# Layer A's dilated keys and group 0's values through DRAM, with GpSimd issuing the moves

## The chip, the cores and the metric

One core of a Trainium2 chip runs the kernel. Its engines are TensorE (PE: matmuls, and transposes as matmuls against an identity), VectorE (DVE), ScalarE (ACT), GpSimd (POOL) and SyncE (SP, which here only issues DMA transfers). Each works through its own instructions in order and waits on semaphores for the others. The metric is the time of one execution on the device in microseconds.

## The reference

Two encoder layers on x (512 tokens, 1024 channels, 16 heads of 64). Each layer is

```
hn = rms_norm(x, norm_gain[i]);  x = x + mixer(hn)
```

Layer A is dilated sliding-window attention: `hn @ w_in` gives, for each of three groups g with dilation 1, 4 and 16, queries, keys and values for all heads, and a gate besides.

```
for g in 0, 1, 2:
    q = rms_norm(qkv[g, 0], q_gain[g]);  k = rms_norm(qkv[g, 1], k_gain[g]);  v = qkv[g, 2]
    # keys at offsets 0, +-d, .., +-reach*d;  reach*d = 64, 256, 1024
    logits = q k^T / 8 + t5_bias;   o_g = softmax(logits) v;   lse_g = log of its denominator
y = sum_g softmax_g(lse_g) * o_g
return (y * silu(gate)) @ w_out
```

Layer B is a two-dimensional neighbourhood attention on an 8 x 64 grid (window 8 x 16, one group) with the same frame. The change is in layer A alone.

## The kernel before

**Tiling.** Every product of a weight with activations is split in two fp32r parts (`wh`, `wl` for the weight, `hn_h`, `hn_l` for the activation) and made of three matmuls (`mm3`). Weights come from DRAM as tiles `wraw` of 1024 columns (three buffers). `split` (L128 to L134) casts each half of one to `wh` on ScalarE and subtracts to `wl` on GpSimd for two tiles in five and on VectorE for the rest; `wh` and `wl` have four buffers each.

**Order.** A layer is a loop over eight pairs of heads, `hc` 0 to 7. `main()` yields TensorE's projections for each pair: first keys and values of groups 1 and 2 (`rawk`, with the values in `v12`), then the three groups' queries and group 0's key (`rawq`), group 0's values (`v0_a`) and the gate (`gate_a`). `side()` holds the attention: `k_a`, `q_a`, `v_a`, `attn_a`. `run` interleaves the two by a clock that counts the nominal time of TensorE's matmuls (213 ns for 512 columns): a side step is taken when its due time, in those nanoseconds after a stamp, has come. `later_on(delay, job)` puts a job on the same clock. TensorE's order is exactly the order of this program (`manual_schedule`); what the other engines do is ordered by a scheduler, except for instructions that `keep_in_program_order` pins.

**Steps that the change touches.**
- `project_qk` copies each accumulator out of PSUM on ScalarE (L477), `squares` squares it on GpSimd (L282, L284) and sums it on VectorE, `head_norm` scales by the root on VectorE (L307), for `rawk` of pairs 1 to 6 by a job 9000 ns later.
- `k_a` transposes the keys of groups 1 and 2 on TensorE, four 128 x 128 transposes a group (L213), and VectorE scales the result into `k12` (L544). `v_a` does the same for group 0's values (`vt`), which ScalarE copies to `v0` (L632).
- For pairs 0 to 5 (`moved`) queries and group 0's key take another way (`turn_q`, `move_q`): VectorE transposes blocks of 32 x 32 in place, SyncE writes the tile to DRAM (`qd`, L595) and reads it back in four parts in which the blocks stand in their new places (`qt`, L601). `split_q` makes the two fp32r parts of query and key.
- In `attn_a` the scores of a pair come in two halves, u = 0 and 1, then the softmax: VectorE minima, ScalarE exponentials (L831) and scaling (L672). The probabilities go back transposed (P^T) in the manner of the queries: `turner.put` transposes blocks on VectorE (L744), `turner.send` writes them to DRAM (`td`, L753) and reads four parts (`pt`, L757), on SyncE. `weigh` multiplies P^T with the values one pair later.
- Pair 6 moves P^T but transposes its queries on TensorE; pair 7 transposes all on TensorE. Layer B uses `turner` too.

Of the kernel before, what the change touches and what calls it, by code (L numbers as in the profile page):

```python
# [42 lines left out]
def tile_hybrid_encoder(  # L43
# [234 lines left out]
    def squares(v, ss, i, ns):  # L278
        sq = wk.tile([P, 512], F32, tag="sq", name="sq")[:, : ns * 64]
        if len(v.shape) == 3:  # L280
            v = v.rearrange("p (a f) r -> p a f r", f=4)
            nc.gpsimd.tensor_mul(sq.rearrange("p (f a r) -> p a f r", f=4, a=4), v, v)  # L282
# [8 lines left out]
    def head_norm(raw, ss, ns, held, delay=0):  # L291


        rs = wk.tile([P, 32], F32, tag="rs", name="rs")
        rsqrt(nc.vector if ns == 8 else nc.gpsimd, rs[:, : 4 * ns], ss[:, : 4 * ns], 4 * ns, 1.0 / DH)

        def scale():
            for i in range(4):
                by = rs[:, i * ns : (i + 1) * ns].unsqueeze(2)
                if len(raw.shape) == 4:  # L300
                    v = raw[:, :, i, :].rearrange("p (h a f) r -> p f h a r", h=2, f=4)
                    by = rs[:, i * ns : (i + 1) * ns].rearrange("p (f h) -> p f h", h=2)
                    by = by.unsqueeze(3).unsqueeze(4).to_broadcast([P, 4, 2, 2, 32])
                else:
# [34 lines left out]
    rs_n = cp.tile([P, 4], F32, name="rs_n")  # L339
    rs_trj = cp.tile([P, S], F32, name="rs_trj")  # L340
    rs_half = cp.tile([P, S], F32, name="rs_half")
# [45 lines left out]
    def scales_a():  # L387
        pa = spread()
        nc.scalar.mul(tjr(rs_half), to_tjr(pa), 0.5)
        nc.scalar.copy(trj(rs_trj), to_trj(pa))  # L390

# [49 lines left out]

    def part(n):
        return rk[:, 1024 * n : 1024 * n + 1024].rearrange("p (i c) -> p i c", i=4)

    def project_qk(n, ns, key, hc, guard, first=False, **kw):
# [3 lines left out]
        def evac(i, acc):  # L449
            if not box:  # L450
# [7 lines left out]
                elif key == "rawk":  # L458
                    box.append(part(0))
                    st["v12", hc] = part(1 + hc % 3)  # L460
                else:
# [7 lines left out]
            elif key == "rawk":  # L469
                pieces = [(raw[:, i, :], acc[:, :256]), (st["v12", hc][:, i, :], acc[:, 256:])]  # L470
            else:
                pieces = [(raw[:, i, :], acc[:, :n])]
            for dst, src in pieces:
                if first:
                    nc.scalar.copy(dst, src)
                else:
                    nc.scalar.activation(dst, src, AF.Copy, scale=rs_n[:, i : i + 1])  # L477
            if not first:
                squares(raw[:, :, i, :] if key == "rawq" and moved(hc) else raw[:, i, : ns * 64], ss, i, ns)

# [8 lines left out]
    def normed(raw, ss, ns, key, hc):  # L489
        head_norm(raw, ss, ns, key == "raw", 9000 if key == "rawk" and 0 < hc < NHC - 1 else 0)  # L490
        if key == "rawq" and moved(hc):
            turn_q(raw)
        st[key, hc] = raw
        stamp[key, hc] = clock[0]

    def first_out():

        raw, ss = st.pop("first")
        for i in range(4):
            for t in (raw, st["v12", 0]):  # L500
                nc.scalar.activation(t[:, i, :], t[:, i, :], AF.Copy, scale=rs_n[:, i : i + 1])
            squares(raw[:, i, :], ss, i, 4)
        normed(raw, ss, 4, "rawk", 0)
# [12 lines left out]
    def v0_a(hc):  # L516
# [3 lines left out]
        vt = wk.tile([P, EXT], F32, tag="vt", name="vt", bufs=1)  # L520
        nc.vector.tensor_mul(trj(vt[:, 64:EXT]), to_trj(acc[0]), trj(rs_trj))
        nc.gpsimd.tensor_copy(vt[:, 0:64], vt[:, EXT - 64 : EXT])
        st["vt", hc] = vt
        stamp["vt", hc] = clock[0]
# [13 lines left out]
    def k_a(hc):  # L538
        yield "wait", ("rawk", hc), 12500 if hc == 0 else 22500 if hc < NHC - 1 else 10000
        k12 = wk.tile([P, 2, 512], F32, tag="k12", name="k12", bufs=1)  # L540
        raw = st.pop(("rawk", hc))
        for g in range(2):
            tp = transpose4(raw, g * P)
            nc.vector.tensor_scalar(k12[:, g, :], tp, gk[:, g + 1 : g + 2], None, op0=ALU.mult)  # L544
            yield
        st["k12", hc] = k12, st.pop(("v12", hc))
        stamp["k12", hc] = 0

    def turn_q(raw):
# [66 lines left out]

    def split_q(q0h, q0l, qt, k0h, k0l):
        src = qt[:, :, 3, :].rearrange("p t (j r) -> p t r j", j=4)
        trj4 = lambda t: t[:, 64:EXT].rearrange("p (t r j) -> p t r j", t=4, j=4)
        tc.keep_in_program_order(nc.scalar.copy(trj4(k0h), src))  # L620
        by_t = lambda t: t.rearrange("p (t x) -> p t x", t=4)
        put_k([(by_t(q0h), by_t(q0l), qt[:, :, 0, :])], 0, True)
        nc.vector.tensor_sub(trj4(k0l), src, trj4(k0h.bitcast(F32)))

    def v_a(hc):
# [4 lines left out]
        for i in range(4):  # L630
            transpose(tp[:, i * P : (i + 1) * P], vt[:, i * P : (i + 1) * P])
        nc.scalar.copy(v0[hc % 2], tp.rearrange("p (i c) -> p i c", i=4))  # L632
        stamp["v", hc] = 0
# [99 lines left out]
    class turner:  # L733
# [11 lines left out]

        def send(self, dst, wait, pace):

# [4 lines left out]
            src = self.t[:, : 4 * run].rearrange("p (b x) -> p b x", b=4)  # L752
            tc.keep_in_program_order(nc.sync.dma_start(d.rearrange("b p x -> p b x"), src))  # L753

            def read(b):
                src = d[b].rearrange("(a k) x -> k a x", a=4)
                tc.keep_in_program_order(nc.sync.dma_start(place[32 * b : 32 * b + 32], src))  # L757
                self.left -= 1
# [4 lines left out]
    def attn_a(hc):  # L763
# [7 lines left out]
        def scores(u):  # L771
# [381 lines left out]
    def side():  # L1153
# [23 lines left out]
        for hc in range(NHC):  # L1177
            if hc < NHC - 1:
                yield from k_a(hc)
                yield from chain(q_a(hc), v_a(hc))  # L1180
                if moved(hc):
                    yield from st.pop(("land", hc))
                yield from attn_a(hc)
                if hc == 1:
# [114 lines left out]
```

## Time and profile before

| | |
|---|---|
| time, median of 3 runs | 851.97 us (850.87 to 852.74) |
| the profiled execution | 852.44 us |
| its span, first to last instruction | 850.6 us |
| TensorE busy | 842.8 us (99%) |
| VectorE, ScalarE, GpSimd busy | 518.5, 431.5, 309.8 us |
| DMA | 141.23 MB, mean 166 GB/s |

The span of the profiled execution is 1.8 us shorter than its time. A matmul's busy time overlaps with the next one's, so a busy TensorE is not one at its peak; what a group of instructions costs is read from the starts of its neighbours. Issuing a DMA does not count as busy. Names such as `acc<-wh,hn_h` mean output and inputs; L209 is the line of the helper through which all matmuls go, L213 that of the transposes.

### The profile page before, as it was taken

What the parts mean: (1) busy time and instruction counts of PE and PEld (TensorE: products, weight loads), DVE (VectorE), ACT (ScalarE), POOL (GpSimd) and SP (SyncE); (2) the same over time, 40 slices, a digit from 0 to 9 for tenths busy, and PEclk for the clock granted to TensorE, in tenths of its full rate; (3) what the DMA queues carried; (4) which work ended last, traced back from release to release, by engine and by line L of the source; (5) the groups of instructions that cost most, each with busy time, mean ns of one, the idle gap of its engine ahead of it and who ended that gap; (6) DMA issues with size and microseconds to landing.
All of it is one profiled execution on the core that took longest, in us unless ns stands there. A gap on an engine that the chain in (4) does not pass through costs nothing.

```text
span 850.6 us, 15397 instructions
## 1 busy us (share of the span) xinstructions
PE 842.8 (99%) x5546; PEld 702.5 (83%) x5546; DVE 518.5 (61%) x1336; ACT 431.5 (51%) x923; POOL 309.8 (36%) x494
## 2 busy tenths in 40 slices
PE   9999999999999999999999999999999999999998
PEld 7788878788788788788788787789998898889786
DVE  7354684684674674674675745447567656766642
ACT  7433653653653653652653554355366655665531
POOL 2252441542541541542531341121354335542511
PEclk9999999999999999999999999999999999999999
DMA  7346377477478378378375562264245664555333
GB/s 250 110 126 216 97 228 227 137 226 241 128 227 248 102 228 243 102 230 246 99 236 159 147 191 79 60 241 146 82 143 138 174 175 148 168 163 158 99 97 127
DMA packets 65228, 141.23 MB, mean 166 GB/s; under 512 B 5760, under 2 KB 23104, under 8 KB 65152
## 3 DMA queue, kind: packets, MB, share of 16 engines
q1 hardware_dynamic: 65008, 139.99, 54.5%
q8 instruction: 44, 0.72, 0.3%
q10 hardware_dynamic: 144, 0.26, 0.1%
q14 instruction: 32, 0.26, 0.1%
HBM read 109.11 MB, written 31.12 MB: 165 GB/s over the span
## 4 chain that ended last, share of the span: by engine, by line
PE 94%; ACT 3%; DVE 1%; DMA 1%; issue 0%; DVEq 0%; ACTq 0%
PE acc L209 80%; PE log L209 5%; PE o L209 5%; PE tp L213 3%; ACT p L1084 1%; ACT p L672 1%; DMA x_all<-in_xt 0%; ACT p L831 0%; ACT wh L128 0%; DVE hn_l L397 0%; ACT rawk L477 0%; DMA eb<-lb_d 0%; PE pa L209 0%; PE pl L209 0%; DVE p L820 0%
## 5 line engine op out<-in xcount | busy, mean ns | idle before, releaser
L128 ACT CAST wh<-wraw 128x512 fp32r<-128x512 f32 (+1 forms) x275 | 161.4, 588 | 294.7 <-PE acc L209 258.0
L209 PE MATMUL acc<-wh,hn_h 128*128 128x512 f32 (+1 forms) x768 | 293.8, 383 | 1.6 <-ACT rawq L477 0.8
L209 PE MATMUL acc<-wh,hn_l 128*128 128x512 f32 (+1 forms) x768 | 285.6, 373 | 0.0
L209 PE MATMUL acc<-wl,hn_h 128*128 128x512 f32 (+1 forms) x768 | 285.5, 373 | 0.0
L134 POOL TENSOR_TENSOR wl<-wraw,wh 128x512 fp32r<-128x512 f32 (+1 forms) x110 | 136.9, 1244 | 361.0 <-ACT wh L128 341.7
L134 DVE TENSOR_TENSOR wl<-wraw,wh 128x512 fp32r<-128x512 f32 (+1 forms) x166 | 111.1, 670 | 141.5 <-ACT wh L128 137.0
L209 PEld LDWEIGHTS acc<-wh,hn_h 128*128 128x128 f32 x768 | 144.6, 188 | 29.2 <-issue 4.9
L209 PEld LDWEIGHTS acc<-wh,hn_l 128*128 128x128 f32 x768 | 144.5, 188 | 20.8
L209 PEld LDWEIGHTS acc<-wl,hn_h 128*128 128x128 f32 x768 | 145.0, 189 | 18.9
L209 PE MATMUL acc<-y,wh 128*128 128x512 f32 x256 | 81.3, 399 | 0.0
L209 PE MATMUL acc<-hn_h,wh 128*128 128x512 f32 x192 | 77.1, 401 | 0.9 <-ACT rawq L477 0.6
L209 PE MATMUL acc<-hn_h,wl 128*128 128x512 f32 x192 | 74.9, 390 | 0.0
L209 PE MATMUL acc<-hn_l,wh 128*128 128x512 f32 x192 | 74.8, 390 | 0.0
L672 ACT ACTIVATE p<-p,mn 128x512 f32<-128x512 f32 (+3 forms) x128 | 69.3, 586 | 0.0
L831 ACT ACTIVATE p<-p,mn 128x512 f32<-128x512 f32 (+1 forms) x64 | 44.8, 701 | 44.7 <-DVE mn L820 44.5
L285 DVE TENSOR_REDUCE ss<-sq 128x4 f32<-128x256 f32 (+1 forms) x96 | 48.4, 505 | 31.2 <-POOL sq L284 19.7
L744 DVE STREAM_TRANSPOSE tr<-p 128x512 f32<-128x512 f32 (+1 forms) x80 | 53.7, 684 | 9.9 <-ACT p L672 9.5
L284 POOL TENSOR_TENSOR sq<-rawk 128x256 f32<-128x256 f32 x64 | 40.3, 637 | 48.2 <-ACT rawk L477 45.1
L209 PEld LDWEIGHTS acc<-y,wh 128*128 128x128 f32 x256 | 46.3, 188 | 10.2 <-issue 1.1
L209 PE MATMUL acc<-y,wl 128*128 128x512 f32 x128 | 50.0, 391 | 0.0
L209 PEld LDWEIGHTS acc<-hn_h,wh 128*128 128x128 f32 x192 | 36.1, 188 | 10.8 <-ACT rawk L477 2.1
L209 PEld LDWEIGHTS acc<-hn_h,wl 128*128 128x128 f32 x192 | 36.0, 188 | 7.8
(138 smaller groups left out, 1038.7 us busy)
## 6 DMA issues: line engine op xcount, KB each, us to landing
wraw<-in_w SPq DMA_DIRECT2D x95, 512.0 KB
wraw<-in_w SPq DMA_DIRECT2D x38, 384.0 KB
td<-tr SPq DMA_DIRECT2D x14, 1024.0 KB
pt<-td SPq DMA_DIRECT2D x56, 256.0 KB
qd<-rawq SPq DMA_DIRECT2D x6, 1024.0 KB
qt<-qd SPq DMA_DIRECT2D x24, 256.0 KB
td<-tr SPq DMA_DIRECT2D x6, 896.0 KB
pt<-td SPq DMA_DIRECT2D x24, 224.0 KB
```

The costliest lines, as they stand in the source:

```text
L128: nc.scalar.copy(h, raw)
L134: eng.tensor_sub(l, raw, h.bitcast(F32))
L209: nc.tensor.matmul(o, l, r, **kw)
L213: nc.tensor.transpose(o, i, ident)
L284: nc.gpsimd.tensor_mul(sq, v, v)
L285: nc.vector.tensor_reduce(ss[:, i * ns : (i + 1) * ns], sq.rearrange("p (a b) -> p a b", b=64), axis=AX.X, op=ALU.add)
L672: nc.scalar.activation(pr, pr, AF.Copy, scale=mn[:, 3:4])
L744: nc.vector.transpose(dst, src[:, :n].rearrange("p (i b k) -> p i b k", b=4, k=32))
L831: nc.scalar.activation(row, row, AF.Exp, bias=mn[:, 1:2], scale=-1.0, accum_out=mn[:, 2:3])
L1084: nc.scalar.activation(pr[:, o : o + n], pr[:, o : o + n], AF.Exp, bias=mn[:, 0:1], scale=-1.0, accum_out=mn[:, 2:3])
```

## The change

- **Keys.** For pairs 0 to 6 (`moved_k`) `rawk` is laid out in blocks of 32, VectorE transposes them in place after the scaling, and `move_k` takes them through DRAM: one write (`kd`) and four reads into `k12`, all issued by GpSimd; then ScalarE scales by the gain. `k_a` with its eight TensorE transposes stays for pair 7.
- **Values of group 0.** For pairs 0 to 5 VectorE transposes `vt` into the last third of the same DRAM tile, which travels with the next pair's keys. GpSimd copies them to `v0`. `v_a` stays for pairs 6 and 7. The scale is that of `rs_half`, doubled later, so `rs_trj` goes.
- **P^T of layer A** is written and read by GpSimd. Its reads are due 15000 ns after the write and 900 apart, before 8500 and 1200.
- **The rest.** `split_q` works in two portions; the fourth square of moved queries is ScalarE's; `q_a`, the scores and `send` get other due times.

```
@@ squares
+            if i == 3:
+                nc.scalar.activation(dst, v, AF.Square)
+            else:
+                nc.gpsimd.tensor_mul(dst, v, v)
@@ head_norm, after the scaling
+            if len(raw.shape) == 5:
+                for g in range(2):
+                    tc.keep_in_program_order(nc.vector.transpose(raw[:, :, g, :, :], raw[:, :, g, :, :]))
@@ normed
+        if key == "rawk" and moved_k(hc):
+            move_k(hc, 17500 if hc else 4000)
@@ v0_a
+        if moved(hc):
+            src = vt[:, :S].rearrange("p (i b x) -> p i b x", i=4, b=4)
+            dst = rk_a[:, :, 256:].rearrange("p b (i x) -> p i b x", i=4)
+            tc.keep_in_program_order(nc.vector.transpose(dst, src))
+            stamp["v", hc] = 0
+            return
@@ new
+    def move_k(hc, delay):
+        n = 384 if hc else 256
+        d = dr.tile([4, P, 384], F32, name="kd", tag="kd", bufs=2)
+        box = []
+        def write():
+            tc.keep_in_program_order(nc.gpsimd.dma_start(d.rearrange("a p y -> p a y")[:, :, :n], rk_a[:, :, :n]))
+            stamp["k12", hc] = 0
+        def read(a):
+            if not box:
+                box.append(wk.tile([P, 4, 384], F32, tag="k12", name="k12", bufs=1))
+            dst = box[0][32 * a : 32 * a + 32, :, :n]
+            src = d[a].rearrange("(b k) y -> k b y", b=4)[:, :, :n]
+            tc.keep_in_program_order(nc.gpsimd.dma_start(dst, src))
+        def landed():
+            kv = box[0]
+            for g in range(2):
+                k = kv[:, :, P * g : P * g + P]
+                tc.keep_in_program_order(nc.scalar.activation(k, k, AF.Copy, scale=gk[:, g + 1 : g + 2]))
+            if hc:
+                src = kv[:, :, 256:].rearrange("p b (i x) -> p b i x", i=4)
+                dst = v0[(hc - 1) % 2].rearrange("p i (b x) -> p b i x", b=4)
+                tc.keep_in_program_order(nc.gpsimd.tensor_scalar(dst, src, 2.0, None, op0=ALU.mult))
+            st["k12", hc] = kv, st.pop(("v12", hc))
+        later_on(delay, write)
+        for n_, a in enumerate((0, 2, 1, 3)):
+            later_on(delay + 16500, partial(read, a))
+        later_on(delay + 29500, landed)
@@ q_a
-        yield "wait", ("rawq", hc), 18000 if moved(hc) else 13000
+        yield "wait", ("rawq", hc), 18000 if moved(hc) else 15000
@@ split_q
-        tc.keep_in_program_order(nc.scalar.copy(trj4(k0h), src))
-        put_k([(by_t(q0h), by_t(q0l), qt[:, :, 0, :])], 0, True)
-        nc.vector.tensor_sub(trj4(k0l), src, trj4(k0h.bitcast(F32)))
+        for k, q in ((slice(0, 3), slice(0, 2)), (slice(3, 4), slice(2, 4))):
+            tc.keep_in_program_order(nc.scalar.copy(trj4(k0h)[:, k], src[:, k]))
+            nc.vector.tensor_sub(trj4(k0l)[:, k], src[:, k], trj4(k0h.bitcast(F32))[:, k])
+            put_k([(by_t(q0h)[:, q], by_t(q0l)[:, q], qt[:, q, 0, :])], 0, True)
@@ turner.send
-        def send(self, dst, wait, pace):
+        def send(self, dst, wait, pace, by=nc.sync):
...
@@ attn_a
-                                k12[hs, g, P * j : P * j + P],
+                                sb(k12[hs], P * g + 32 * j, [[384, 4], [1, 32]]),
...
-                    yield "wait", ("rawk", hc + 1), 5200 if u == 0 else 16800
+                    yield "wait", ("rawk", hc + 1), 7000 if u == 0 else 16800
...
-                send = partial(turned.send, pq[:, 2048 * u : 2048 * u + 2048], 8500, 1200)
-                later_on(7000 + 2000 * u, send)
+                send = partial(turned.send, pq[:, 2048 * u : 2048 * u + 2048], 15000, 900, nc.gpsimd)
+                later_on(7000 + 3000 * u, send)
@@ side
-                yield from k_a(hc)
-                yield from chain(q_a(hc), v_a(hc))
+                yield from q_a(hc)
                 if moved(hc):
                     yield from st.pop(("land", hc))
+                else:
+                    yield from v_a(hc)
```

More of the change, by code (lines that the diff above doesn't have):

```diff
@@ L440, in tile_hybrid_encoder, with part @@
     moved = lambda hc: hc < NHC - 2
-    def part(n):
-        return rk[:, 1024 * n : 1024 * n + 1024].rearrange("p (i c) -> p i c", i=4)
+    moved_k = lambda hc: hc < NHC - 1
+    rk_a = rk[:, :1536].rearrange("p (a y) -> p a y", a=4)
+    def part(o):
+        return rk[:, o : o + 1024].rearrange("p (i c) -> p i c", i=4)
     def project_qk(n, ns, key, hc, guard, first=False, **kw):
@@ L469, in evac @@
             elif key == "rawk":
-                pieces = [(raw[:, i, :], acc[:, :256]), (st["v12", hc][:, i, :], acc[:, 256:])]
+                keys = raw[:, i, :], acc[:, :256]
+                if moved_k(hc):
+                    keys = raw[:, :, :, i, :], acc[:, :256].rearrange("p (g a x) -> p a g x", g=2, a=4)
+                pieces = [keys, (st["v12", hc][:, i, :], acc[:, 256:])]
             else:
@@ L477, in evac @@
                     nc.scalar.activation(dst, src, AF.Copy, scale=rs_n[:, i : i + 1])
-            if not first:
-                squares(raw[:, :, i, :] if key == "rawq" and moved(hc) else raw[:, i, : ns * 64], ss, i, ns)
+            if first:
+                return
+            if key == "rawk" and moved_k(hc):
+                v = raw[:, :, :, i, :]
+            elif key == "rawq" and moved(hc):
+                v = raw[:, :, i, :]
+            else:
+                v = raw[:, i, : ns * 64]
+            squares(v, ss, i, ns)
         tile_of = lambda hn: lambda k, i: hn[:, k, P * i : P * (i + 1)]
@@ L492, in normed @@
             turn_q(raw)
+        if key == "rawk" and moved_k(hc):
+            move_k(hc, 17500 if hc else 4000)
         st[key, hc] = raw
@@ L499, in first_out @@
         for i in range(4):
-            for t in (raw, st["v12", 0]):
-                nc.scalar.activation(t[:, i, :], t[:, i, :], AF.Copy, scale=rs_n[:, i : i + 1])
-            squares(raw[:, i, :], ss, i, 4)
+            for t in (raw[:, :, :, i, :], st["v12", 0][:, i, :]):
+                nc.scalar.activation(t, t, AF.Copy, scale=rs_n[:, i : i + 1])
+            squares(raw[:, :, :, i, :], ss, i, 4)
         normed(raw, ss, 4, "rawk", 0)
@@ L520, in v0_a @@
         vt = wk.tile([P, EXT], F32, tag="vt", name="vt", bufs=1)
-        nc.vector.tensor_mul(trj(vt[:, 64:EXT]), to_trj(acc[0]), trj(rs_trj))
+        in_trj = lambda t, order: t.rearrange(f"p ({order}) -> p t r j", t=4, j=4)
+        nc.vector.tensor_mul(
+            in_trj(vt[:, 64:EXT], "t r j"), in_trj(acc[0], "j t r"), in_trj(rs_half, "t j r")
+        )
         nc.gpsimd.tensor_copy(vt[:, 0:64], vt[:, EXT - 64 : EXT])
+        if moved(hc):
[3 more added lines that the diff above has]
+            stamp["v", hc] = 0
+            return
         st["vt", hc] = vt
@@ L538, in k_a @@
     def k_a(hc):
-        yield "wait", ("rawk", hc), 12500 if hc == 0 else 22500 if hc < NHC - 1 else 10000
-        k12 = wk.tile([P, 2, 512], F32, tag="k12", name="k12", bufs=1)
+        yield "wait", ("rawk", hc), 10000
+        k12 = wk.tile([P, 4, 384], F32, tag="k12", name="k12", bufs=1)
         raw = st.pop(("rawk", hc))
@@ L631, in v_a @@
             transpose(tp[:, i * P : (i + 1) * P], vt[:, i * P : (i + 1) * P])
-        nc.scalar.copy(v0[hc % 2], tp.rearrange("p (i c) -> p i c", i=4))
+        nc.scalar.mul(v0[hc % 2], tp.rearrange("p (i c) -> p i c", i=4), 2.0)
         stamp["v", hc] = 0
```

25 lines of the change are left out of this document (17 added, 8 removed).

## The prediction

> **What bounds the kernel now.** I read the page first (busy shares, granted clock, chain), then TensorE's waits.
>
> ```profile
> span 850.6 us, 15397 instructions
> PE 842.8 (99%) x5546; PEld 702.5 (83%) x5546; DVE 518.5 (61%) x1336; ACT 431.5 (51%) x923; POOL 309.8 (36%) x494
> PEclk9999999999999999999999999999999999999999
> PE 94%; ACT 3%; DVE 1%; DMA 1%; issue 0%; DVEq 0%; ACTq 0%
> ...
> PE acc L209 <- ACT rawq L477: 1.4, 2, 0.8
> ```
>
> TensorE is busy for 99% of the span at a full granted clock, and the chain that ended last runs through it for 94%. Its longest wait is 1.4 us in all, in two places, both for the copies of the queries out of PSUM. So the time falls by what TensorE no longer does, less the waits that appear instead. All other engines have room on average; the question is where they have none.
>
> **What the change removes from TensorE.** The keys of head pairs 0 to 6 no longer need two groups of four transposes each (14 groups), and the group-0 values of pairs 0 to 5 no longer one (6 groups): 80 of the transposes in the two rows below.
>
> ```profile
> L213 PE MATMUL tp<-ident,rawk 128*128 128x128 f32 x128 | 19.1, 272 | 0.0
> L213 PE MATMUL tp<-ident,vt 128*128 128x128 f32 x32 | 4.8, 272 | 0.0
> ```
>
> Busy time is no price here, because matmuls overlap. The order of time gives it; columns are start, duration, engine, line, operation. The last two rows, from the chain in order of time, give the pitch of plain matmuls and the period of a head pair (306.57 - 242.45 = 64.1 us).
>
> ```profile
> 73.79 0.39 PE L209 MATMUL acc<-wh,hn_l 128*128 128x512 f32 x1
> 74.02 0.60 PE L213 MATMUL tp<-ident,vt 128*128 128x128 f32 x4
> 74.38 0.48 PE L209 MATMUL acc<-wh,hn_h 128*128 128x512 f32 x1
> 74.69 0.40 PE L209 MATMUL acc<-wl,hn_h 128*128 128x512 f32 x1
> 74.92 0.40 PE L209 MATMUL acc<-wh,hn_l 128*128 128x512 f32 x1
> 75.16 0.40 PE L209 MATMUL acc<-wh,hn_h 128*128 128x512 f32 x1
> ...
> 242.45 22.47 PE acc L209 x99
> ...
> 306.57 22.47 PE acc L209 x99
> ```
>
> 99 matmuls in 22.47 us are 0.227 us each. From 73.79 to 75.16 stand four such matmuls and one group: 1.37 - 4 x 0.227 = 0.46; the slowness of the next two matmuls adds 0.01, so 0.47 a group. 20 groups are **9.4 us**, all on the path.
>
> The score matmuls now read keys in four runs of 32 columns instead of one of 128. I cost this at nothing, as the weighing already reads P^T in such runs; either sign would be small.
>
> **What grows at the two waits for queries.** In both places TensorE runs ahead of ScalarE's softmax, and the code now brings the two closer together. First pair 0:
>
> ```profile
> 114.31 0.60 PE L213 MATMUL tp<-ident,rawk 128*128 128x128 f32 x4
> ...
> 116.22 0.50 PE L209 MATMUL acc<-hn_h,wh 128*128 128x512 f32 x1 [0.62 <-ACT rawq L477]
> ```
>
> The transposes at 114.31 lie between the scores and the wait; without them TensorE arrives 0.47 us earlier and ScalarE ends no sooner. Cost **0.5 us**. Then pair 6:
>
> ```profile
> 462.31 0.36 PE L209 MATMUL log<-k0h,q0h 64*128 64x192 f32 x2
> 464.31 0.50 PE L209 MATMUL acc<-wh,hn_h 128*128 128x512 f32 x1
> 468.98 0.39 PE L209 MATMUL acc<-wh,hn_l 128*128 128x512 f32 x1
> 470.14 0.50 PE L209 MATMUL acc<-wh,hn_h 128*128 128x512 f32 x1 [0.77 <-ACT rawq L477]
> ...
> 465.04 0.67 ACT L831 ACTIVATE p<-p,mn 128x448 f32<-128x448 f32 x1 [2.69 <-DVE mn L820]
> 466.36 0.66 ACT L672 ACTIVATE p<-p,mn 128x448 f32<-128x448 f32 x1
> 466.92 0.71 ACT L831 ACTIVATE p<-p,mn 128x512 f32<-128x512 f32 x1
> 469.41 0.68 ACT L477 ACTIVATE rawq<-acc,rs_n 128x512 f32<-128x512 f32 x1
> ```
>
> Scores begin at S = 462.31, plain matmuls 2.0 later; 21 of them follow before TensorE needs an emptied bank, which is late by 0.9 us (468.98 + 0.23 to 470.14). In the changed order only 12 stand there (2.7 us), so it needs the four banks from S + 4.7 on, at one per 0.7. ScalarE can begin its exponentials at S + 2.73 as now. In its new order stand two of them, one evacuation, a scaling, an evacuation, two exponentials, a scaling, two evacuations. At some 0.65 apiece the last bank is free at S + 9.1, and three matmuls more end at S + 9.9 instead of S + 7.4. A wait of 2.4 takes the place of 0.9: **1.5 us** lost. If ScalarE is ahead, this costs nothing; if VectorE's part of the softmax slips, a microsecond more.
>
> Sum: -9.4 + 0.5 + 1.5 = **-7.4 us**, if nothing else reaches TensorE.
>
> **The moves, and what covers them.** For every pair 0 to 6, GpSimd issues one key write and four reads, and two P^T writes and eight reads that SyncE issued before: 105 issues. SyncE's price of the same P^T issues (shortest, median, longest in ns) and GpSimd's crowded stretch in pair 3 are
>
> ```profile
> L757 SPq DMA_DIRECT2D pt<-td x80: 313/423/1899, 110.0 to 776.9; - x80
> L753 SPq DMA_DIRECT2D td<-tr x20: 377/382/427, 104.2 to 762.9; - x20
> ...
> 247.33 1.29 POOL L134 TENSOR_TENSOR wl<-wraw,wh 128x512 fp32r<-128x512 f32 x1
> 248.59 1.49 POOL L282 TENSOR_TENSOR sq<-rawq 128x512 f32<-128x512 f32 x1
> 251.46 0.77 POOL L522 COPY vt<-vt 128x64 f32<-128x64 f32 x1 [1.38 <-DVE vt L521]
> 253.87 1.29 POOL L134 TENSOR_TENSOR wl<-wraw,wh 128x512 fp32r<-128x512 f32 x1 [1.64 <-ACT wh L128]
> 253.17 0.62 ACT L128 CAST wh<-wraw 128x512 fp32r<-128x512 f32 x1 [1.76 <-DVE rs L116]
> ```
>
> The square at 248.59 goes to ScalarE. In its place, between the weight subtractions of 247.33 and 253.87, now stand the second P^T write, four P^T reads, the copy (0.77) and four key reads. What is queued behind them is the weight remainder `wl`, and TensorE waits for that. Its latest start: there are four `wh` and four `wl` buffers, so the cast at 253.17 began when TensorE let the tile four back go; three tiles of 12 matmuls (8.2 us) later, at 261.3, it turns to this one, and needs the remainder 0.23 later. Less 1.29 for the subtraction: 260.3. GpSimd is free at 248.6, so the stretch may take **11.7 us**.
>
> No row shows an issue on GpSimd. SyncE's 0.42 bounds it from below; a full pass of GpSimd, 1.29, is the nearest row above; holding GpSimd until the data land is the far end (5 to 12 us, next rows). I take 0.86, the middle of the near two, since one is the same transfer and the other the same engine. Then 9 x 0.86 + 0.77 = 8.5: no wait. At 1.29 it is 12.4: 0.7 lost in each of six stretches (pairs 1 to 6), 4 us.
>
> The page "DMA: Bandwidth & Descriptors" of the Trainium skill (section "Issuing engine by pattern") gives plain loads and stores to SyncE, and under "Specifications" puts the first byte at about 1 us from GpSimd against 0.6 from SyncE; at 1 us an issue, an estimate from that page, the stretch takes 9.8 us and the sum stays.
>
> A second wait lies in the same stretch. The changed program counts GpSimd's transfers on eight semaphores in turn, so the last key read waits until the P^T write sent eight transfers earlier has landed. The same write on SyncE, from its issue to the first read that waits for it:
>
> ```profile
> 230.62 0.38 SPq L753 DMA_DIRECT2D td<-tr  x1
> 235.91 0.80 SPq L757 DMA_DIRECT2D pt<-td  x2
> 244.63 0.38 SPq L753 DMA_DIRECT2D td<-tr  x1
> 255.27 0.79 SPq L757 DMA_DIRECT2D pt<-td  x2
> 372.82 0.38 SPq L753 DMA_DIRECT2D td<-tr  x1
> 384.81 0.79 SPq L757 DMA_DIRECT2D pt<-td  x2
> ...
> 245.00:250.00 5.00, 5.00 (x23) 4.13 (x23) 2.85 (x4) 2.06 (x4) 5.00 (x5) 1.00 0.90 210
> 250.00:255.00 5.00, 5.00 (x23) 4.13 (x22) 4.57 (x12) 1.25 (x2) 1.98 (x3) 1.00 0.89 329
> ```
>
> It took at most 5.3, 10.6 and 12.0 us. With the last issue (0.86) it may take 10.8 before TensorE waits. The long ones had a weight load and two P^T reads, 1 MB, ahead of them in SyncE's queue; GpSimd's queue has nothing ahead of this write. I take 8, between 5.3 and 10.6. The last two rows (engines, clock, DMA share, GB/s) show that there is little room: the DMA engines are 90% busy there.
>
> The rest is covered. VectorE loses the key scalings and gains two transposes a pair for keys and one for values, about one pass more, at 61% busy. ScalarE gains two key scalings and a square and loses a copy, under 2 us of each pair's 64, at 51%; a cast late by that much is within the same lead as above (some 6 us). The keys' reads come 13 us before their scaling is due, by the code's own due times. The halves of `split_q` run before scores that are themselves set 1.8 us later. SyncE's weight loads no longer stand behind P^T waits; TensorE waits for no weight now, so that is worth nothing. Without this cover, ScalarE's 2 us would cost up to 12 over six pairs.
>
> **The rivals.** *The two waits do not grow* (ScalarE keeps up): -9.4, 842.6 on the scale of the median. *An issue costs GpSimd a full pass*: 4 us lost, 848.6. For it: the engine itself does the work; against it: the 0.42 of the same transfer.
>
> *The landing of the P^T write becomes the bound*, the slower side. Each microsecond beyond 10.8 costs six. At 13, which takes the 12.0 of the third row and the 0.79 MB of keys that now share the 90% busy engines, 2.2 x 6 = 13 us are lost: 857.8. It decides from 12.0 on. For it: that row; against it: the empty queue.
>
> *VectorE holds GpSimd up*: if each issue waits out a VectorE instruction of 0.7 us (VectorE is busy for 4.57 of 5 us in the last row), 9 x 0.7 = 6.3 go on top of 8.5; 3.1 over in six stretches is 19 us, 863. Against it: the subtraction beside that same VectorE work takes its 1.29. The page "SBUF — State Buffer", section "Who interferes with whom", of the Trainium skill has such a lock, for copies, casts and scalar operations in a two-port mode; no run here shows it on an issue.
>
> That the change does not do what it says I exclude: the 80 transposes are gone from the program.
>
> **How the numbers follow.** The profiled execution took 852.44 us, 1.8 more than its span, and lies 0.5 above the median of 851.97. The sum on it gives 845.0; on the median, which I predict, **844.6**. Chances: forecast 0.47, no growth 0.10, dear issues 0.12, landing 0.23, VectorE 0.08. Faster by over 0.2% (1.7 us, about what a measurement of this kernel can tell from no change): the first two and 0.10 of dear issues, 0.67. Within: 0.02 of these and 0.04 of landing, 0.06. Slower: 0.19 of landing and VectorE's 0.08, 0.27. The range reaches from 841.8, just under no growth, to 858, the landing case; beyond lie the VectorE case and the longest landings. The forecast's own range is 843 to 846.5.
>
> **What would show it.** Right: 20 groups of transposes missing, the pairs' period shorter by 1.4 us from 64.1, TensorE's waits for `rawq` at 3 to 4 us and no wait for `wl`. Wrong: TensorE waiting for GpSimd's `wl` once in every pair (issues or landing, told apart by whether GpSimd stands before the last key read), or for P^T, keys or values.

## The result and the profile after

| | time, median | ratio to before, 95% interval |
|---|---|---|
| before, in the same runs | 852.36 us (850.87 to 853.47) | |
| after | **863.55 us** (860.88 to 866.03) | 1.0131 (1.0114 to 1.0149) |

The change makes the kernel slower by 11 us, where 844.6 was forecast and the range ended at 858. The profiled execution took 865.35 us. The same lines of its page as were shown of before:

```profile
span 863.6 us, 15352 instructions
PE 844.2 (98%) x5466; PEld 698.2 (81%) x5466; DVE 528.5 (61%) x1354; ACT 438.8 (51%) x948; POOL 365.3 (42%) x599
PEclk9999999999999999999999999999999999999999
...
PE 72%; DVE 9%; DMA 8%; ACT 6%; SPq 2%; POOL 2%; issue 2%; ACTq 0%; DVEq 0%; POOLq 0%
PE acc L209 62%; PE log L209 5%; DMA qd<-rawq 3%; DMA qt<-qd 3%; PE o L209 3%; PE tp L213 2%; DVE wl L134 1%; ACT p L910 1%; ACT p L751 1%; DMA wraw<-in_w 1%; ACT wh L128 1%; ACT p L1163 1%; SPq L791 1%; DVE rawq L317 1%; SPq L678 1%
```

The 80 transposes are gone (5546 to 5466 matmuls). GpSimd's 105 issues, unlike SyncE's, are counted here as busy instructions (x494 to x599). But the chain that ended last runs through TensorE for 72% in place of 94%, and what came in is named: the write and the reads of the moved queries, `qd<-rawq` and `qt<-qd`, 3% each. Those two transfers are not part of the change. The totals of the waits (who waits and for what; then us in all, number of times, longest) say where they bite; the last two rows are from TensorE's own list:

```profile
DVE k0l L701 <- ACT k0h L700: 26.2, 5, 6.4
ACT k0h L700 <- DMA qt<-qd: 25.9, 5, 6.4
ACT wh L128 <- DMA wraw<-in_w: 19.8, 7, 6.9
...
PE log L209 <- DVE gt L771: 3.9, 5, 0.8
PE acc L209 <- ACT rawq L500: 3.0, 3, 1.6
```

Before, ScalarE never waited for `qt`. Now it does in each of pairs 1 to 5, 5 us on average. Pair 3 shows how this reaches TensorE, before and then after, in the order of time:

```profile
264.29 0.43 SPq L595 DMA_DIRECT2D qd<-rawq  x1
270.70 1.75 SPq L601 DMA_DIRECT2D qt<-qd  x4
279.71 1.18 ACT L620 CAST k0h<-qt 128x512 fp32r<-128x512 f32 x1
285.51 0.36 PE L209 MATMUL log<-k0h,q0h 64*128 64x192 f32 x2
285.92 0.30 PE L209 MATMUL log<-k0h,q0h 64*128 64x256 f32 x2
...
286.39 1.18 PE L209 MATMUL log<-k,qt 64*32 64x128 f32 x64
```

```profile
267.11 0.43 SPq L672 DMA_DIRECT2D qd<-rawq  x1
280.36 1.75 SPq L678 DMA_DIRECT2D qt<-qd  x4
286.87 0.91 ACT L700 CAST k0h<-qt 128x384 fp32r<-128x384 f32 x1 [4.28 <-DMA qt<-qd]
288.92 0.36 PE L209 MATMUL log<-k0h,q0h 64*128 64x192 f32 x2
289.34 0.30 PE L209 MATMUL log<-k0h,q0h 64*128 64x256 f32 x1
289.67 0.70 DVE L771 TENSOR_TENSOR gt<-gt,o 128x512 f32<-128x512 f32 x1
290.43 0.38 PE L209 MATMUL log<-k0h,q0h 64*128 64x256 f32 x1 [0.79 <-DVE gt L771]
...
290.97 1.18 PE L209 MATMUL log<-k,qt 64*32 64x128 f32 x64
```

The reads `qt` wait for the landing of the write `qd`: 270.70 - 264.29 = 6.4 us before, 280.36 - 267.11 = 13.3 us after. So the queries' split starts 2.0 us ahead of the scores where it had 5.8. VectorE then does its share of the split just before the gate's product `gt` (L771), and the last tile of the first half's plain scores waits for that product (290.43), which stands behind the split in VectorE's order. (Scores and `o` share four PSUM banks in the program, and the fourth score tile needs the one from which the product reads `o`.) The other pairs look alike: from the first score matmul to the first one with dilated keys (`log<-k,qt`) TensorE took 0.9 us in every pair before, and 2.9, 2.7, 2.0, 2.7 and 2.7 us in pairs 1 to 5 after.

What the DMA engines did in the 40 us before these scores (queue: packets, MB, share of the 16 engines), before and after:

```profile
q1 hardware_dynamic: 3811, 8.96, 75.9%
```

```profile
q1 hardware_dynamic: 2683, 6.66, 56.1%
q0 software_dynamic: 1168, 3.93, 36.9%
```

76% became 93%. Over the whole execution 141.23 MB became 151.71, and the 10.48 MB between are exactly the moved keys and values, written and read: six pairs of 2 x 0.786 and one of 2 x 0.524.

### The profile page after: what moved, and what is told of

The parts are those of the page before. It is cut to its first block, busy times and chain, and to the rows that moved or that the text cites. A ratio compares the mean times of both kernels' runs of the same rounds, so it can differ in the third digit from the quotient of the medians.

```text
span 863.6 us, 15352 instructions
## 1 busy us (share of the span) xinstructions
PE 844.2 (98%) x5466; PEld 698.2 (81%) x5466; DVE 528.5 (61%) x1354; ACT 438.8 (51%) x948; POOL 365.3 (42%) x599
## 2 busy tenths in 40 slices
DMA packets 61084, 151.71 MB, mean 176 GB/s; under 512 B 6320, under 2 KB 23664, under 8 KB 61008
## 4 chain that ended last, share of the span: by engine, by line
PE 72%; DVE 9%; DMA 8%; ACT 6%; SPq 2%; POOL 2%; issue 2%; ACTq 0%; DVEq 0%; POOLq 0%
PE acc L209 62%; PE log L209 5%; DMA qd<-rawq 3%; DMA qt<-qd 3%; PE o L209 3%; PE tp L213 2%; DVE wl L134 1%; ACT p L910 1%; ACT p L751 1%; DMA wraw<-in_w 1%; ACT wh L128 1%; ACT p L1163 1%; SPq L791 1%; DVE rawq L317 1%; SPq L678 1%
## 5 line engine op out<-in xcount | busy, mean ns | idle before, releaser
L134 DVE TENSOR_TENSOR wl<-wraw,wh 128x512 fp32r<-128x512 f32 (+1 forms) x166 | 116.6, 703 | 143.8 <-ACT wh L128 139.5
L209 PEld LDWEIGHTS acc<-hn_l,wh 128*128 128x128 f32 x192 | 36.1, 188 | 6.8
```

The source lines that it names most:

```text
L134: eng.tensor_sub(l, raw, h.bitcast(F32))
L209: nc.tensor.matmul(o, l, r, **kw)
```

## The experiments

The theory after the result: **crowding**. The bytes of the key moves share the DMA engines with the moved queries, which land late. Rival A: it is GpSimd's issuing, its order and its semaphores. Rival B: it is the added work and order on ScalarE and VectorE (halves of `split_q`, the square, due times). Each group of runs below shared its runs of the kernel before (851.0 to 852.4 us), with which the ratios are formed. A difference from after's 863.55 us compares two groups; formed with the ratios it can come out up to 3 us otherwise.

**P^T back on SyncE** (pt_sync):

```
- send = partial(turned.send, ..., 15000, 900, nc.gpsimd);  later_on(7000 + 3000 * u, send)
+ send = partial(turned.send, ..., 8500, 1200);             later_on(7000 + 2000 * u, send)
```

> The changed kernel with P^T of layer A sent by SyncE again, at the old due times (7000 + 2000 u, 8500, 1200). Theory 1 (crowded DMA engines: P^T reads, now due 6 to 8 us later, and the key reads lie beside the moved queries, whose qt<-qd lands up to 6.4 us late, and TensorE waits for the scores' operands): only the 0.75 MB of key reads (some 3 us at 250 GB/s) stay beside the queries, ScalarE's wait for qt falls from 4 to 6.4 us to under 2.5, time 850 to 857. Rival A (it is GpSimd's issuing that costs: its order, its eight semaphores): nearly the whole loss goes, 843 to 848. Rival B (the new order and the extra work on ScalarE and VectorE, halves of split_q, square, due times): 861 to 865.

857.93 us, ratio 1.0084 (1.0065 to 1.0103): 5.6 us better than after (4.0 by the ratios), still 7 slower than before. Rival A as sole cause is out. But the queries' wait did not fall as the theory said:

```profile
ACT k0h L700 <- DMA qt<-qd: 22.2, 5, 5.0
```

The write now lands in 8.2 to 9.0 us in pairs 2 to 5, but is issued some 4 us later after the queries leave PSUM (21.4 to 22.1 us in place of 17.2 to 18.7), as it stands behind P^T and weights in SyncE's queue.

**P^T early, by GpSimd** (pt_early):

```
- send = partial(turned.send, ..., 15000, 900, nc.gpsimd);   later_on(7000 + 3000 * u, send)
+ send = partial(turned.send, ..., 8500, 1200, nc.gpsimd);   later_on(7000 + 2000 * u, send)
```

> The changed kernel with P^T still sent by GpSimd, but at the old due times (7000 + 2000 u, 8500, 1200). Theory 1: as with SyncE, since only the time of the transfers counts: 850 to 857, unless GpSimd, held by the P^T write's landing, sends them late again. Rival A: 861 to 866, GpSimd's issues are all there and wait longer for the landing of the write. Rival B: 861 to 865.

868.76 us, 1.0229 (1.0170 to 1.0287): worse by 5 than after, above the ranges of all three theories, and 10.8 above pt_sync, from which it differs in the issuing engine alone. The queries' wait fell (18.2 us in all for 25.9), but weights now land late, ScalarE's cast of them waits up to 10.1 us, and the gate's copy behind that cast holds TensorE up:

```profile
PE acc L209 <- ACT gt L543: 8.1, 4, 4.8
```

**Key reads 8.5 us earlier** (k_early):

```
- later_on(delay + 16500, partial(read, a));  later_on(delay + 29500, landed)
+ later_on(delay + 8000, partial(read, a));   later_on(delay + 25000, landed)
```

> The changed kernel with the key reads due 8.5 us earlier (8000 in place of 16500 after the write; the scaling 4500 earlier), so that they lie before the second P^T and not beside the queries. Theory 1: 0.75 MB leaves the queries' stretch, qt lands some 3 us earlier in pairs 1 to 5: TensorE's waits at the scores fall by 1 to 1.5 us a pair, 855 to 860. Rivals A and B: 862 to 866.

870.13 us, 1.0226 (1.0186 to 1.0267). The theory's number was wrong. In pair 3 the reads did leave earlier (26.0 us after the first scores of pair 2, 32.7 in after), yet the queries' write still took 12.7 us to land, and now the weights are late too (63.7 us of ScalarE's waiting in all, 19.8 in after). Moving the bytes in time freed nothing here. Why it costs 6.6 us more than the change itself is not settled.

**P^T alone** (pt_alone), on the kernel before:

```
- send = partial(turned.send, ..., 8500, 1200);             later_on(7000 + 2000 * u, send)
+ send = partial(turned.send, ..., 15000, 900, nc.gpsimd);  later_on(7000 + 3000 * u, send)
```

> The kernel before with one part of the change: P^T of layer A sent by GpSimd at the new due times (7000 + 3000 u, 15000, 900); keys and values by TensorE as before. Theory 1: the P^T reads (1 MB of them after the queries' write is due) now lie beside the moved queries, qt lands 3 to 5 us later than before and the scores wait in pairs 1 to 5: 855 to 861. Rival A: 853 to 862, with TensorE waiting for wl or GpSimd. Rival B: 851 to 853, as before.

858.53 us, 1.0083 (1.0063 to 1.0104). In size as the theory said, but by another way, and that is rival A's: pairs 1 to 5 keep their 64.1 us and `k0h` waits 4.6 us in all; 6 us are lost in one place, ahead of pair 6. There GpSimd issues a write and four reads before it squares the last quarter of pair 6's queries, which VectorE's sum, root and scaling and then TensorE's transposes wait for (the last row is a window: busy PE, PEld, DVE, ACT, POOL, granted clock, DMA share, GB/s):

```profile
439.44 0.80 POOL L753 DMA_DIRECT2D td<-tr  x1
440.23 2.19 POOL L757 DMA_DIRECT2D pt<-td  x4
442.44 1.29 POOL L284 TENSOR_TENSOR sq<-rawq 128x512 f32<-128x512 f32 x1
...
452.49 2.28 PE L213 MATMUL tp<-ident,rawq 128*128 128x128 f32 x4 [2.15 <-DVE rawq L307]
...
452.40:459.00 6.60, 6.13 (x17) 4.37 (x18) 2.59 (x6) 1.27 (x2) 1.41 (x3) 0.50 0.91 216
```

The issues delay the square by 3.0 us, TensorE waits 2.2, and behind that it ran 6.6 us at half clock, which cost another 3.3. In the whole change the fourth square of pairs 0 to 5 is on ScalarE, but pair 6's is not, and the same stands there: its four transposes wait for `rawq` one by one, 1.8 us in all, and pair 7's for `rawk`, whose squares stand behind P^T issues too, 1.35.

**The bytes alone** (traffic): the kernel before, which computes all as before, plus a write and four reads of a key move's size in pairs 1 to 5, for which nobody waits; the reads go to another buffer in DRAM. In short:

```
+ nc.gpsimd.dma_start(kd, hn_h[:, 0:3, :])          # 0.79 MB, due 17500 after the keys
+ for a in (0, 2, 1, 3): nc.gpsimd.dma_start(sink_a, kd_a)   # due 16500 later
```

> The kernel before, computing all as before, plus transfers that nobody waits for: in pairs 1 to 5 GpSimd writes 0.79 MB to DRAM and reads it back in four pieces into another DRAM buffer, at the due times of the key moves (17500 after the keys, reads 16500 later). Theory 1, sharpened by the last runs (the bytes of the key moves themselves, not their time or their queue, delay the moved queries): 1.57 MB at some 250 GB/s are 6.3 us of all 16 DMA engines in a stretch that is 76 to 97% busy; the wait of k0h for qt rises from nothing to 2 to 5 us a pair and TensorE waits at the scores, 855 to 862. Rival A (GpSimd's issues hold up what it computes): TensorE waits for wl, 853 to 860. Rival B (the added work and order on ScalarE and VectorE): 851 to 853, as before.

855.00 us, 1.0042 (1.0027 to 1.0057). No transpose was taken away and no result is waited for, yet the kernel is 2.9 us slower, and the queries are what is late:

```profile
ACT k0h L642 <- DMA qt<-qd: 8.5, 5, 3.7
```

That is the lower edge of what was expected. There is slack before this hurts: 1.3 us were lost at pair 2's scores, with the 3.7, and 0.2 at pair 4's. Most of the rest, 0.9 us, lies behind the last scores of layer A, where nothing was added, and is not explained.

**The same instructions without the bytes** (few_bytes): all five transfers of each move stay with their order and waits, but carry a quarter of the rows and of the columns; `k12` is one buffer, zeroed at the start.

```
- nc.gpsimd.dma_start(d[:, :, :n], rk_a[:, :, :n]);  ... dma_start(dst[:, :, :n], src[:, :, :n])
+ nc.gpsimd.dma_start(d[:32, :, :96], rk_a[:32, :, :96]);  ... dma_start(dst[:, :1, :96], src[:, :1, :96])
```

> The changed kernel with every transfer of the key moves issued as before by GpSimd, with the same waits and the same order, but cut to a quarter of its rows and at most 96 columns of them: under 1/12 of the bytes (most of the moved keys and values are left out, and zeros from the start of the program stand in their place). Theory 1 (the bytes): the queries' write lands in 6 to 9 us in place of 12 to 15, k0h's wait for qt falls from 5 us a pair to under 1.5, the waits at the scores and the wait for late weights at the start go: 846 to 853. Rivals A (issues and waits on GpSimd) and B (work and order on ScalarE and VectorE): 860 to 865.

851.00 us, 0.9991 (0.9978 to 1.0004): **12.5 us of the time after are the bytes of the moves** (11.9 by the ratios). The queries' write lands in 7.5 to 11.1 us in pairs 1 to 5, better than in after and less well than the 6 to 9 expected, and ScalarE's wait for their reads falls from 25.9 us in all:

```profile
ACT k0h L702 <- DMA qt<-qd: 11.6, 5, 5.6
```

From the chain in order of time, the scores' starts in pairs 3, 4 and 5:

```profile
286.24 2.00 PE log L209 x75
...
349.13 2.00 PE log L209 x75
...
412.01 2.00 PE log L209 x75
```

They are 62.9 us apart, 64.1 before: the forecast's 62.7 within 0.2, with nothing at the scores. What is left over lies elsewhere: in pair 1 the queries still came late, which cost 3 us with a slow clock behind it, and pair 6's transposes wait 1.6 us for the late square. (The profiled execution, 853.24 us, was the longest of ten.) The run computes with zeros for most keys and values and has its key reads land sooner too. It does not show by itself that neither matters; but TensorE waits for no key in after, and traffic and v_by_pe (below), which leave nothing out, point the same way.

**The same with P^T on SyncE** (few_bytes_sync), with the edit of pt_sync besides:

> The changed kernel with the bytes of the key moves cut as in the run before (most of the keys and values left out), and P^T of layer A by SyncE at the old due times. If P^T on GpSimd makes the rest of the loss (pair 1's queries land 4 us late, 3 us lost with the slow clock behind it; the queries of pair 6 scaled late, 1.5 us): 844 to 848. If the rest lies in the due times of the last pairs alone: 849 to 852.

846.96 us, 0.9947 (0.9926 to 0.9968). So P^T on GpSimd at its new due times costs another 4.0 us (both places just named are gone, and TensorE's wait in pair 1 is down to 0.3), and with both gone the kernel is 5.1 us faster than before; 2.4 us are left to the forecast.

**The smaller edits** (old_split):

```
- for k, q in ((slice(0, 3), slice(0, 2)), (slice(3, 4), slice(2, 4))):  ...
+ copy(trj4(k0h), src);  put_k([... qt[:, :, 0, :]], 0, True);  tensor_sub(trj4(k0l), src, ...)
- if i == 3: nc.scalar.activation(dst, v, AF.Square)
+ nc.gpsimd.tensor_mul(dst, v, v)                                # all four
```

> The changed kernel with split_q in one portion and all four squares of the queries on GpSimd, as before. Theory 1: these parts do not make the loss; the late queries now reach the first scores some 1 us later in pairs 1 to 5 as they are no longer split in two, 863 to 869. Rival B: 853 to 860.

862.43 us, 1.0129 (1.0103 to 1.0155). Rival B is out as far as it lies in the halves and the square; the due times and the rest of the added work stay, but few_bytes keeps them too and is 12.5 us faster. That the halves gain something was wrong, it is the same time. The way to it tells something: with the square on GpSimd the queries' write is issued some 3.5 us later after the queries leave PSUM (20.9 to 21.0 in pairs 2 to 5, 17.2 to 18.7 in after), and its landing comes at the same moment all the same (30.5 to 31.8 us, in after 30.6 to 31.8). So issuing the write earlier did not bring its landing forward; that the transfers ahead of it set the moment fits, but was not shown separately.

**A third of the bytes less** (v_by_pe), values of group 0 by `v_a` on TensorE as before:

```
- n = 384 if hc else 256
+ n = 256
...                              # vt is neither transposed by VectorE nor copied by GpSimd
- yield from q_a(hc)
+ yield from chain(q_a(hc), v_a(hc))
```

> The changed kernel with the values of group 0 turned by TensorE as before (6 groups of transposes return, 6 x 0.47 = 2.8 us); keys alone are moved, 256 columns in place of 384, so 0.5 MB less in each pair. Theory 1: qt lands some 2 us earlier in pairs 1 to 5, the waits at the scores fall by half, and with the 2.8 us the time is 858 to 863. Rivals A and B: the transposes come on top, 865 to 868.

859.10 us, 1.0095 (1.0061 to 1.0129). 4.4 us better than after, which the two intervals do not tell from nothing; but six groups of transposes came back (2.8 us), and 7 us under that sum is clear of noise: that is what 0.5 MB less a pair is worth (6 us by the ratios). The queries' wait fell from 25.9 to 16.1 us, and four of the five pairs lost at most 0.3 us at the scores.

**First and last pair without moves** (mid), with `k_a` for pairs 0 and 6 and `v_a` for pair 5:

```
- moved_k = lambda hc: hc < NHC - 1
+ moved_k = lambda hc: 0 < hc < NHC - 2
```

> The changed kernel with keys moved in pairs 1 to 5 only; pairs 0 and 6 and the values of pair 5 by TensorE (5 groups of transposes return, 2.4 us). Theory 1: no key write beside the first weights, so the wait of 1.7 us at 67.6 us goes; in pair 6 the projection's wait for an emptied bank falls from 1.75 us with its slow clock behind it to 0.9: 859 to 863. If the moves of pairs 0 and 6 cost nothing: 865 to 867.

866.74 us, 1.0176 (1.0160 to 1.0193), 3.2 more than after. The wait at 67.6 us, behind weights that came late beside pair 0's key write, is gone as expected:

```profile
67.85 1.14 ACT L128 CAST wh<-wraw 128x512 fp32r<-128x512 f32 x2 [6.91 <-DMA wraw<-in_w]
...
69.52 0.50 PE L209 MATMUL acc<-wh,hn_h 128*128 128x512 f32 x1 [1.54 <-ACT gt L543]
```

(rows of after). Yet nothing of it reached the end: pairs 1 and 2 now wait longer, with slower clocks. What was won ahead of the late queries was waited out there.

**Later scores** (scores_late), to give the queries time:

```
- yield "wait", ("rawk", hc + 1), 7000 if u == 0 else 16800
+ yield "wait", ("rawk", hc + 1), 10000 if u == 0 else 16800
```

> The changed kernel with the first scores of pairs 1 to 5 due 3000 later (10000 after the next keys in place of 7000), nothing else. Theory 1: TensorE does projection matmuls in the 3 us in which it now waits for the split queries and the emptied bank; the waits at the scores (some 9 us in five pairs) go, 853 to 858. If the softmax, the P^T moves and the rest merely slip by as much, 860 to 866. Rival B: no change, 862 to 865.

878.08 us, 1.0309 (1.0270 to 1.0349), and the theory's number is far off. The waits at the scores shrink, but the softmax runs later and ScalarE empties the next queries' banks behind it; TensorE waits for that 15.8 us in 8 places, where it was 3.0 us in 3 in after. The scores stand between two limits: the landing of this pair's queries, and the evacuation of the next pair's.

**Combinations.** mid_pt_sync_late has the edits of mid and pt_sync and the first scores due at 9000:

```
- yield "wait", ("rawk", hc + 1), 7000 if u == 0 else 16800
+ yield "wait", ("rawk", hc + 1), 9000 if u == 0 else 16800
```

> A combination: the changed kernel with keys moved in pairs 1 to 5 only (pairs 0 and 6 by TensorE; 4 groups of keys and 1 of values return, 2.4 us), P^T by SyncE at the old due times, and the first scores due 2000 later. Theory 1: the start (2.2 us of waiting for the gate's copy, behind late weights) is as before, the waits at the scores are mostly gone: 847 to 853. Without theory 1: 858 to 862, the transposes on top of the 857.9 of the kernel with P^T on SyncE.

875.25 us, 1.0274 (1.0247 to 1.0301), by the same evacuations (17.6 us of TensorE's waiting). mid_keys_sync has the edits of mid, pt_sync and v_by_pe (keys alone, in pairs 1 to 5, P^T on SyncE) and the scores as in the change:

> A combination that gives up what crowds: keys alone moved and in pairs 1 to 5 only (10 groups, 4.7 us saved), values by TensorE, P^T by SyncE at the old due times. Theory 1: 1.05 MB more in each of five pairs in place of 1.57, no P^T late; the queries' wait falls to 1 to 3 us a pair, waits at the scores to some 2 us in all, 848 to 854. Without theory 1: 858 to 862.

853.85 us, 1.0022 (1.0001 to 1.0043). q6_due is that with the queries of pairs 6 and 7 due as before:

```
- yield "wait", ("rawq", hc), 18000 if moved(hc) else 15000
+ yield "wait", ("rawq", hc), 18000 if moved(hc) else 13000
```

> The combination with keys alone moved in pairs 1 to 5, values by TensorE and P^T by SyncE, and the queries of pair 6 due at 13000 again in place of 15000. If that due time makes the wait of 1.75 us (0.9 before) for an emptied bank in pair 6: 1 to 1.5 us under the 853.9 of that combination, 851 to 853. If it does not: 853 to 855.

**849.58 us, 0.9975 (0.9963 to 0.9988)**: the one complete version that beats both kernels, by a quarter of a per cent. TensorE's waits for emptied query banks are 2.0 us in all, longest 1.2, for 2.9 and 1.6 in mid_keys_sync. The gain of 4.3 us is more than the 1 to 1.5 expected: among the executions with a granted clock of 0.999 or more it is 1.7 us (849.4 for 851.1), and a lower clock, which six of the ten of mid_keys_sync had, came in one of twelve here. Last, keys_1_to_5 has the scores due as before as well:

```
- yield "wait", ("rawk", hc + 1), 7000 if u == 0 else 16800
+ yield "wait", ("rawk", hc + 1), 5200 if u == 0 else 16800
```

> The same with the first scores due at 5200 again in place of 7000, so that only 10 groups of key transposes, the key moves themselves and the smaller edits are left of the change. If the queries still land in time (slack of 3 us in pairs 1 to 5 at 7000): pair 0's wait shrinks by 0.5 us, 849 to 852, at or just below the kernel before. If the earlier scores meet the late queries, each microsecond counts five times: 854 to 860.

853.93 us, 1.0022 (1.0004 to 1.0041): the earlier scores meet the queries again (`k0h` waits 18.3 us in all, 14.0 in q6_due, each in the longest of twelve executions).

## Why the prediction was wrong, step by step

- **The transposes, 9.4 us.** Right within 0.2 us a pair. Where the bytes are gone, a pair's period falls from 64.1 to 62.9 us, 1.2 for the 1.4 forecast.
- **GpSimd's crowded stretch.** Right in outcome, in size by luck:

```profile
252.45 0.79 POOL L832 DMA_DIRECT2D td<-tr  x1
253.24 1.11 POOL L836 DMA_DIRECT2D pt<-td  x2
255.14 0.73 POOL L557 COPY vt<-vt 128x64 f32<-128x64 f32 x1 [0.79 <-DVE vt L554]
255.82 1.10 POOL L836 DMA_DIRECT2D pt<-td  x2
256.91 1.64 POOL L608 DMA_DIRECT2D k<-kd  x3
260.15 0.55 POOL L608 DMA_DIRECT2D k<-kd  x1 [1.60 <-DMA td<-tr]
260.72 1.30 POOL L134 TENSOR_TENSOR wl<-wraw,wh 128x512 fp32r<-128x512 f32 x1
```

  From the first issue to `wl` are 8.3 us, forecast 8.5. But an issue costs 0.55 for a read and 0.79 for a write, for the 0.86 taken, which with the copy makes 5.9; two waits that the 8.5 did not hold, for `vt` (0.8) and for the P^T write's landing (1.6), make up the rest. That landing took 7.7 us (252.45 to 260.15), for the 8 taken, and TensorE waits for no `wl`. But the step named `wl` as all that is queued behind, and took pair 3 for all of them. In pair 6 the square is still behind these issues, as told above: 1.8 us there and 1.35 in pair 7.
- **The rivals.** Dear issues, the landing and VectorE's hold, 43 chances in 100, all had GpSimd's `wl` late; the loss was not there, and none of the signs that were to show the prediction wrong appeared: TensorE waits for no `wl`, P^T, key or value. None had the transfers that were in the stretch already.
- **The two waits for queries.** Right, with sizes within 0.4. In pair 0 TensorE's pause grew from 0.8 to 1.35 us over its pace (forecast 0.5 more). In pair 6 it has 0.34 and 1.75 in place of 0.93, 1.2 more (forecast 1.5); the slow clock behind the second, another 1.7 us (last section), was not forecast:

```profile
116.90 0.50 PE L209 MATMUL acc<-hn_h,wh 128*128 128x512 f32 x1 [1.19 <-ACT rawq L500]
...
477.95 0.50 PE L209 MATMUL acc<-wh,hn_h 128*128 128x512 f32 x1 [0.17 <-ACT rawq L500]
...
480.49 0.50 PE L209 MATMUL acc<-wh,hn_h 128*128 128x512 f32 x1 [1.58 <-ACT rawq L500]
```

- **"The rest is covered" is the step that failed.** It asked whether the moved keys come in time for themselves and never what their bytes do to the transfers beside them. The text had the row that shows it (DMA engines 90% busy) and used it for one transfer only, the P^T write. Even the keys came later than their 13 us of lead allowed, though TensorE waits for none of them:

```profile
POOL v L618 <- DMA k<-kd: 17.9, 5, 5.4
...
ACT k L614 <- DMA k<-kd: 13.3, 5, 3.3
```

  The transfer that lost the most was one that the change does not touch: the queries' write, 13.3 us for 6.4 in pair 3, and the reads behind it. Taking the bytes out is worth 12.5 us (few_bytes). The starts of the scores of pairs 1 and 5, in after and then in few_bytes, say how much of that lies at the queries:

```profile
157.96 0.35 PE L209 MATMUL log<-k0h,q0h 64*128 64x192 f32 x2 [0.19 <-ACT q0h L718]
...
419.18 0.35 PE L209 MATMUL log<-k0h,q0h 64*128 64x192 f32 x2
```

```profile
157.33 0.35 PE L209 MATMUL log<-k0h,q0h 64*128 64x192 f32 x2
...
411.94 0.36 PE L209 MATMUL log<-k0h,q0h 64*128 64x192 f32 x2
```

  Between them few_bytes gains 6.6 us, and 1.8 at pair 5's own scores: 8.4 of the 12.1 us between the two profiled spans. Of the rest 1.0 lies ahead of pair 0's scores, beside the late weights, and 2.9 between pair 6's and pair 7's, where no queries are moved; the slow clock behind 480.49 and the 1.35 us of pair 7's transposes are in after alone. Put into the kernel before, the bytes of five moves cost only 2.9 us (traffic): the price depends on the slack that the rest of the change leaves. The page "DMA: Bandwidth & Descriptors" of the Trainium skill has the rule in its section "Issuing engines are not separate DMA queues": DMAs that different engines start run on the same 16 DMA engines and interleave. The trace agrees (36.9% of the engines' time went to GpSimd's queue in that stretch, and SyncE's write doubled), and it speaks against this change; the prediction cited that page for the issuing engine and not for this.
- **"SyncE's weight loads no longer stand behind P^T waits ... worth nothing", and P^T on GpSimd at no cost but the crowded stretch.** That cost is wrong too. In SyncE's queue P^T, weights and queries stood in one line; from two queues they share the engines (56.1% and 36.9% of the engines' time above). With the squares behind the issues that costs 4.0 us without the keys' bytes (few_bytes to few_bytes_sync), 5.6 with them (after to pt_sync); how much is the queue and how much the squares was not separated.
- **"The halves of `split_q` run before scores that are themselves set 1.8 us later."** Wrong: they run 2.0 us before the scores, as the data were not there. As edits they cost nothing (old_split).

So 863.55 - 844.6 = 19.0 us come apart as 12.5 (bytes of the moves), 4.0 (P^T's queue) and 2.4 left open; of the last, few_bytes_sync shows 1.0 us of waiting at 67.1 us and 1.1 at the scores of pairs 1 and 2. Taking out P^T first gives 5.6 for it and 11.0 for the bytes; by the ratios P^T is worth 3.7 and 4.0 in the two orders, so a difference between them is not shown.

## What to carry to other kernels

Before bytes are added to a stretch whose DMA engines are mostly busy (76% here), list every transfer already in it, with the time from its issue to the first instruction that waits for it and the slack that is left there, and add the new bytes to each; here most of the loss showed at a transfer with little slack, not at the new one. Taking work from the engine that is busy all the time pays only if what replaces it has room of its own: here 9.4 us of transposes were bought with 10.5 MB. When two transfers must share, an order in one queue can beat two queues (pt_sync against pt_early), and a smaller move (keys alone, five pairs) won where the whole one lost.

## What the runs showed of the hardware

TensorE's clock dropped after waits that are short. These are windows of after (the granted clock is the third number from the end), behind the scores of pair 1 and behind the wait at 480.49:

```profile
160.00:163.50 3.50, 3.39 (x71) 2.69 (x72) 1.47 (x10) 1.43 (x2) 2.48 (x3) 0.54 0.02 5
...
481.00:484.50 3.50, 3.50 (x21) 2.60 (x22) 2.91 (x5) 2.38 (x5) 2.79 (x3) 0.52 0.00 0
```

The longest single wait ahead of them was 0.8 us (in a stretch that took 2.9 us for 0.9 before, from 157.96 on) and 1.6 us. At a clock of 0.54 and 0.52 over 3.5 us they cost 1.6 and 1.7 us of time. It does not follow every such wait: few_bytes has the wait of 1.75 us in pair 6 too, and full clock behind it. The page "TensorE: Matmul & The Clock Gate" of the Trainium skill, section "Why this matters for your kernels", asks to avoid gaps of over some 3 us; here less was enough. The 40 slices of the page do not show it (all 9), as a slice is 21.6 us long.
